# A decoder layer on one core: the value projection begins first, and the four pool weight groups are fused between its tiles 1 to 5

## The chip, the cores and the metric

The kernel runs on one core of one Trainium2 chip. The metric is the device time of one execution in microseconds (us). Three runs of the kernel before gave 2354.69, 2355.07 and 2358.67 us; their median, 2355.07 us, is the time before. A core has five engines with queues of their own: TensorE (PE in the profile; its weight loads are PEld), VectorE (DVE), ScalarE (ACT), GpSimd (POOL) and SyncE (SP), which here only issues DMAs. Each engine works through its queue in order and waits on semaphores for the others.

## The reference

One layer of a hybrid decoder. 16 meta tokens go ahead of 2048 tokens of width 1024, all are layer-normed, and one projection gives q, k, v, the forget logits, two gates and the pool input. Attention with a forget bias and a causal pooling run side by side, are gated, and go through one output projection and a second layer norm. What the change touches is the first norm, the v columns of the projection and the pool's per-group weights:

```python
h = jnp.concatenate([meta, x], axis=1)
h = layer_norm(h, ln_in_g, ln_in_b)
...
h = jnp.einsum('bld,dc->blc', x, w_in)
q, k, v, f_logit, g_att, u, g_pool = jnp.split(h, SPLITS, axis=-1)
...
    outs.append((hi - lo) / cnt - u32[:, :, sl])
d = jnp.stack(outs, axis=2)
y = jnp.einsum('blgc,gce->blge', d, w_pool.astype(jnp.float32))
```

The trailing mean is linear, so the kernel multiplies the pool input's columns of `w_in` by `w_pool` ahead of time, group by group, and projects straight into the mapped channels. This is the fusing that the change moves: for each of the four groups a 1024 x 256 matrix times a 256 x 256 one.

## The kernel before

**Numbers in two parts.** All products are in fp32 built from two parts: `split` writes a high part with ScalarE (`hi`) and the remainder, source less high part, with VectorE (`lo`), or with GpSimd where the call says so. `mm3` then issues three matmuls (high x high, high x low, low x high). Low x low is left out.

**Order.** The class `Ordered` chains the instructions of TensorE, VectorE, ScalarE and GpSimd to the order in which the code issues them. SyncE is not chained: the framework's scheduler sets the order of the DMAs. All five queues then run in order. A tile taken from a pool with `bufs=n` waits until the tile n turns earlier has been read. Nearly every instruction is recorded through one helper, so the profile gives nearly all of them line 86; they are told apart by their tiles.

**The stage that the change touches**, in the order of the code:

1. Fusing. `fuse_load` brings the weights of all four groups into tiles of their own (`wp`: 256 x 256; `wu`: two of 128 x 1024), `fuse_split` makes the parts `ph`, `pl`, `uh`, `ul`, and `fuse_mm` issues 48 matmuls of 256 columns a group into four PSUM tiles `d`, which ScalarE and VectorE copy in turn to `o` (or `vs`) for the DMA to `wupd`. The splits of the next group, the norms of the first three token tiles and the splits of the value weights `wv` (`wvh`, `wvl`) are placed between the four.
2. The first value half. Tokens are held transposed in `hh` and `hl` (high and low part, 8 slabs of 128 channels by 2064 tokens each). `ln_norm(i)` normalises token tile i (statistics `bst` and `mv` on VectorE, the root `rs` on ScalarE, `rs` and `nb` on VectorE, the scaling of `xt` on ScalarE, then gain and bias on GpSimd), `ln_turn(i)` transposes it on TensorE into `tr` and splits `tr` into `hh` and `hl`. `v_tile(0, wts, i)` multiplies 128 tokens by 512 value columns: 8 channel slabs times three matmuls of 512 columns into one of two tiles `d`; ScalarE and VectorE split that into `vs`, a DMA takes it to `vd`. In step i of the loop stand the transposes of token tile i + 1, the norm of i + 3 and value tile i. Value tile i needs token tiles i - 1 and i, since the 16 meta tokens shift them. There are 16 tiles of 128 tokens and a 17th of 16 tokens, for which the same 24 matmuls are issued.
3. The second value half: the weights of the other 512 columns are loaded to three tiles `wst` and split, and 17 value tiles follow without transposes.
4. The forget logits `zc`, then the jobs of the projections, the attention and the output; the change leaves them alone.

Of the kernel before, what the change touches and what calls it, by code (L numbers as in the profile page):

```python
# [9 lines left out]
F32 = mybir.dt.float32  # L10
# [30 lines left out]
def kernel(  # L41
# [147 lines left out]
    with ExitStack() as vscope:  # L189
        vpool = pool(vscope, "vpool")  # L190
# [21 lines left out]
        def ln_norm(i):  # L212
# [11 lines left out]
            nc.vector.scalar_tensor_tensor(  # L224
                out=nb[:n], in0=mv[:n, 0:1], scalar=-1.0, in1=rs[:n], op0=ALU.mult, op1=ALU.mult
            )
            nc.scalar.activation(
                out=xt[:n], in_=xt[:n], func=AF.Identity, scale=rs[:n], bias=nb[:n]
            )
            for op, row in ((ALU.mult, g_bc), (ALU.add, b_bc)):  # L230
                nc.gpsimd.tensor_tensor(out=xt[:n], in0=xt[:n], in1=row[:n], op=op)
# [26 lines left out]
        def v_tile(half, wts, kt):  # L258
            n = min(P, L - P * kt)
            ps = dense()  # L260
            sl = slice(P * kt, P * kt + n)
            for k in range(KT):
                mm3(ps[:n], hh[:, k, sl], hl[:, k, sl], wts[k][0], wts[k][1], k == 0, k == KT - 1)
            vs = vslot().rearrange("p (h a e) -> p h a e", h=8, a=2)
            pv = ps[:n].rearrange("p (h e) -> p h e", e=DH)
            split(vs[:n, :, 1, :], vs[:n, :, 0, :], pv)
# [5 lines left out]
        fscope = ExitStack()  # L272
        fz = pool(fscope, "fz", side="right")

        def fuse_load(g):
            wp = fz.tile([P, 2, 256], F32, tag="wp", name="wp", bufs=4)
            dma(wp, wpool[g])
            us = [wp]
            for k in range(2):
                us.append(fz.tile([P, D], F32, tag="wu", name="wu", bufs=8))  # L280
                dma(us[-1], wut[2 * g + k])
            return us

        def fuse_split(us, r):
            def one(i, u):
                shape, tag = ([P, 2, 256], "p") if i == 0 else ([P, D], "u")
                h_, l_ = (
                    fz.tile(shape, F32R, tag=tag + t, name=tag + t, bufs=2 if i == 0 else 4)
                    for t in "hl"
                )  # L290
                split(h_, l_, u, nc.gpsimd if i == 2 else None)
                r.append((h_, l_))

            return [lambda i=i, u=u: one(i, u) for i, u in enumerate(us)]

        def fuse_mm(g, ws, us, pieces):
            raw = [
                f32(vslot()) if g == 3 else fz.tile([P, D], F32, tag="o", name="o", bufs=6)
                for _ in range(2)
            ]  # L300
            os = [t.rearrange("p (k b e) -> p k b e", k=4, b=2) for t in raw]
            n = -(-len(pieces) // 4)

            def evac(kp, ps):
                pv = ps.rearrange("p (a b e) -> p a b e", a=2, b=2)
                dst = os[kp // 2][:, 2 * (kp % 2) : 2 * (kp % 2) + 2]
                if kp % 2:
                    nc.vector.tensor_copy(dst, pv)
                else:
                    nc.scalar.copy(out=dst, in_=pv)  # L310

            last = None
            for kp in range(4):
                ps = dense()
                for s in range(2):
                    dsl = slice(P * (2 * kp + s), P * (2 * kp + s + 1))
                    for k in range(2):
                        mm3(
                            ps[:, 256 * s : 256 * (s + 1)], us[k][0][:, dsl], us[k][1][:, dsl],
                            ws[0][:, k], ws[1][:, k], k == 0, k == 1,  # L320
                        )
                if last:
                    evac(*last)
                last = (kp, ps)
                for f in pieces[n * kp : n * (kp + 1)]:
                    f()
            evac(*last)
            for b in range(2):
                for q in range(2):
                    dma(wupd[2 * g + b][:, 4 * q : 4 * q + 4, :], os[q][:, :, b, :])  # L330
# [3 lines left out]
        raws = {0: fuse_load(0)}  # L334
        ln_load(-1)
        raws[1] = fuse_load(1)
# [3 lines left out]
        raws[2] = fuse_load(2)  # L340
        ln_load(1)
        raws[3] = fuse_load(3)
        ln_load(2)
        sts = deque()
        for k in range(KT):
            sts.append(fz.tile([P, 512], F32, tag="wv", name="wv", bufs=KT))
            dma(sts[-1], wv[0, k])
        dma(wfs, wf)
        dma(bf_t, b_forget)
        dma(psc_t, pool_scale)  # L350
        hot = []
        for f in fuse_split(raws.pop(0), hot):
            f()
        wts = []
        for g in range(4):
            us = hot
            ws = us.pop(0)
            hot = []
            pieces = []
            if g + 1 < 4:  # L360
                pieces += fuse_split(raws.pop(g + 1), hot)
                pieces.append(lambda: ln_norm(g - 1))
            if g >= 2:
                pieces += [lambda: wts.append(wv_split(sts.popleft()))] * 4
            fuse_mm(g, ws, us, pieces)
        fscope.close()
        htp = pool(phase_a, "htp", side="right")
        hh = htp.tile([P, KT, L], F32R, tag="hh", name="hh")
        hl = htp.tile([P, KT, L], F32R, tag="hl", name="hl")
        ln_turn(-1)  # L370
        ln_load(3)
        ln_turn(0)
        ln_norm(2)
        split(wfr[:, :, 0:H], wfr[:, :, 32 : 32 + H], wfs)
        for i in range(NKT):
# [8 lines left out]
            if i == 16:  # L384
                wts1 = [wv_split(sts.popleft())]
                sts.append(wv_load(1, 3))
            v_tile(0, wts, i)
            if i == 15:
                lnscope.close()
                wq = pool(phase_a, "wq", side="right")  # L390
        wts = wts1
        for k in range(1, KT):
            wts.append(wv_split(sts.popleft()))
            if k + 3 < KT:
                sts.append(wv_load(1, k + 3))
        for kt in range(NKT):
# [4 lines left out]
            v_tile(1, wts, kt)  # L401

# [826 lines left out]
```

## Time and profile before

| what | value |
| --- | --- |
| median of three runs | 2355.07 us |
| the profiled execution: time, span of its trace | 2353.42 us, 2351.7 us |
| granted TensorE clock over that execution | 0.994 of full |
| span busy: TensorE, VectorE, ScalarE, GpSimd | 97%, 64%, 41%, 30% |
| first value matmul, its place in the span | 56.87 us |
| transposes of token tile 6 (step 5 of the loop) begin | 91.01 us |

The span and the profiled time differ by 1.7 us, which lie outside the trace. A row of the timeline has the start, the busy time, the engine, the line, the operation, what is written from what is read with its shape, the count (xN), and in brackets the idle time ahead of it with what ended it. The busy time of one matmul is longer than the distance between the starts of two, because they are pipelined: the distance is what a stream of them costs. A row of the stretches has the bounds, the length, the busy time of each engine with the count of instructions, the granted clock, the share of time that the DMA engines were busy, and GB/s. A row of the chain of waits has a start, a length, and what the chain that ended last was doing there.

### The profile page before, as it was taken

Reading aid. Unit: us, or ns where it says so; the run is one execution under the profiler, and the core shown is the slowest. Engines: PE = TensorE matmul, PEld = TensorE weight load, DVE = VectorE, ACT = ScalarE, POOL = GpSimd, SP = SyncE. Lnnn points to the kernel's source line nnn. Section 1 sums busy time; section 2 is a strip of 40 time slices with the busy share of each in tenths; the row PEclk is TensorE's granted clock in tenths of the full one; section 3 lists DMA queues with packets and bytes.
Section 4 is the critical chain, followed back from the end, with each engine's and each line's share of the span. In section 5 each row is a group of like instructions: output and inputs, shape, how many; then the busy total and the mean of one; then the engine's idle time right before and its main releaser. Section 6 shows DMA issues by size and latency. Waiting matters only on the chain.

```text
span 2351.7 us, 32595 instructions
## 1 busy us (share of the span) xinstructions
PE 2289.3 (97%) x11450; PEld 1924.1 (82%) x11450; DVE 1501.9 (64%) x2372; ACT 959.9 (41%) x1813; POOL 716.8 (30%) x528
## 2 busy tenths in 40 slices
PE   6999999999999999999999999999999999998998
PEld 5878799999999999999888677777777777776787
DVE  6641146755766567656634488778788878877357
ACT  4431221212212212121111587777778777776000
POOL 4740021212313414140001235444453544444000
PEclk8999999999999999999999999999999999999999
DMA  7853222222222222222212857566666667555965
GB/s 252 265 175 90 69 90 70 84 63 92 91 62 91 78 70 91 62 95 80 82 65 71 219 170 226 162 210 175 186 189 187 208 173 228 169 164 164 300 193 165
DMA packets 317507, 333.59 MB, mean 142 GB/s; under 512 B 27744, under 2 KB 241072, under 8 KB 317312
## 3 DMA queue, kind: packets, MB, share of 16 engines
q1 hardware_dynamic: 317344, 331.51, 46.2%
q8 instruction: 91, 1.49, 0.3%
q14 instruction: 72, 0.59, 0.1%
HBM read 207.43 MB, written 124.00 MB: 141 GB/s over the span
## 4 chain that ended last, share of the span: by engine, by line
PE 89%; DVE 3%; DMA 3%; ACT 2%; issue 2%; POOL 1%; SPq 0%; DVEq 0%; ACTq 0%; POOLq 0%
PE d L86 61%; PE s L86 11%; PE yo L86 7%; PE mx L86 6%; PE xo L86 5%; POOL tu L86 1%; DVE pl L86 1%; PE tr L86 1%; ACT ph L86 1%; POOL araw L86 1%; DMA wst<-in_wout_dram 0%; ACT s L86 0%; DMA wu<-in_wut_dram 0%; DMA g_bc<-in_ln_in_g_dram 0%; DVE acc L86 0%
## 5 line engine op out<-in xcount | busy, mean ns | idle before, releaser
L86 PE MATMUL d<-hh,wh 128*128 128x412 f32 (+2 forms) x1472 | 543.8, 369 | 0.0
L86 PE MATMUL d<-hl,wh 128*128 128x412 f32 (+2 forms) x1472 | 538.2, 366 | 0.0
L86 PE MATMUL d<-hh,wl 128*128 128x412 f32 (+2 forms) x1472 | 537.9, 365 | 0.0
L86 DVE TENSOR_TENSOR pl<-s,ph 128x512 fp32r<-128x512 f32 (+2 forms) x576 | 375.4, 664 | 147.0 <-ACT s L86 134.2
L86 DVE TENSOR_REDUCE mxs<-mx 128x1 f32<-128x912 f32 (+14 forms) x416 | 359.5, 865 | 85.6 <-PE mx L86 75.8
L86 ACT ACTIVATE ph<-s 128x512 fp32r<-128x512 f32 (+2 forms) x576 | 335.2, 582 | 170.1 <-PE s L86 157.8
L86 PE MATMUL d<-wh,xm 128*128 128x512 f32 x1024 | 352.1, 400 | 4.5 <-DMA xm<-xa 3.7
L86 ACT ACTIVATE s<-s 128x512 f32<-128x512 f32 (+2 forms) x576 | 332.7, 578 | 0.0
L86 PEld LDWEIGHTS d<-hl,wh 128*128 128x128 f32 x1472 | 277.6, 189 | 24.8
L86 PEld LDWEIGHTS d<-hh,wh 128*128 128x128 f32 x1472 | 276.8, 188 | 23.2
L86 PEld LDWEIGHTS d<-hh,wl 128*128 128x128 f32 x1472 | 276.6, 188 | 23.4
L86 PE MATMUL s<-qa,ka 68*128 68x512 f32 (+4 forms) x704 | 257.9, 367 | 19.1 <-DVE pl L86 18.8
L86 POOL TENSOR_TENSOR wl<-wst,wh 128x1024 fp32r<-128x1024 f32 x40 | 96.3, 2407 | 571.4 <-ACT wh L86 545.8
L86 PE MATMUL s<-qb,kb 128*128 128x512 f32 (+4 forms) x704 | 244.8, 351 | 0.0
L86 PE MATMUL xo<-ph,vt 128*128 128x512 f32 (+3 forms) x640 | 232.7, 367 | 0.0
L86 POOL TENSOR_TENSOR tu<-ph 128x512 f32<-128x512 f32 x144 | 191.2, 1330 | 135.3 <-ACT ph L86 118.8
L86 PEld LDWEIGHTS d<-wh,xm 128*128 128x128 f32 x1024 | 192.3, 189 | 42.3 <-issue 2.9
L86 PE MATMUL yo<-pl,vt 128*66 128x512 f32 (+3 forms) x640 | 223.3, 365 | 1.1 <-ACT c L86 1.1
L86 PE MATMUL d<-wl,xm 128*128 128x512 f32 x512 | 204.3, 399 | 0.0
L86 PE MATMUL mx<-ka,qa 66*128 66x512 f32 (+5 forms) x704 | 197.9, 347 | 3.4 <-ACT qa L86 3.4
L86 PEld LDWEIGHTS s<-qa,ka 68*128 68x128 f32 (+1 forms) x704 | 127.8, 182 | 73.3 <-DVE pl L86 31.1
L86 DVE TENSOR_TENSOR mx<-mx,mask_q 128x128 f32<-128x128 f32 x256 | 76.6, 299 | 117.4 <-PE mx L86 115.0
(140 smaller groups left out, 3091.5 us busy)
## 6 DMA issues: line engine op xcount, KB each, us to landing
xm<-xp SPq DMA_DIRECT2D x32, 1024.0 KB
xm<-xa SPq DMA_DIRECT2D x20, 1024.0 KB
vd<-vs SPq DMA_DIRECT2D x32, 512.0 KB
vt<-vd SPq DMA_DIRECT2D x64, 256.0 KB
qb<-kqd SPq DMA_DIRECT2D x64, 256.0 KB
xa<-am SPq DMA_DIRECT2D x32, 512.0 KB
xp<-pm SPq DMA_DIRECT2D x32, 412.0 KB
kqd<-lo SPq DMA_DIRECT2D x64, 206.0 KB
```

The costliest lines, as they stand in the source:

```text
L86: return in_order(f(*a, **k))
```

## The change

The norm and the value projection now stand first, and `hh` and `hl` are allocated at the start.

- **Start.** The queue of loads begins with the meta tokens, token tile 0, the gain and bias rows and the eight value weights, which land in tiles that are free at that time (`wst`, a tile of the `xt` pool called `wraw`, and both `vs`). The norms of the meta tokens, of token tiles 0 and 1 have gain and bias on VectorE; from token tile 2 on GpSimd has them as before.
- **Fusing.** Step i of the loop, for i = 1 to 4, holds the transposes of token tile i + 1 (in step 1 those of tile 2 come behind the value tile), the norm of token tile i + 2, `fuse_feed(i - 1)`, value tile i, and `fuse_mm(i - 1)`. `fuse_feed` loads a group as five pieces of 128 x 512 (0: `w_pool`; 1 and 2: the first slab's two halves; 3 and 4: the second's) through the three tiles `wst`, so the load of piece 3 waits for the split of piece 0 and that of piece 4 for the split of piece 1. The parts go to the last 1024 token columns of `hh` and `hl`, which no token tile needs before step 7. Every low part is VectorE's. `fuse_mm` has the same 48 matmuls a group in two PSUM tiles `fz` of 1024 columns: the first half needs pieces 0, 1 and 3, the second 0, 2 and 4. ScalarE copies each half to a `vs` tile.
- **Norms.** In step 5 two norms are made up (tiles 7 and 8); later steps have that of i + 3 as before.
- **16-row tiles.** `v_rest` takes the place of the 17th value tile of each half: `hs` holds the 16 tokens' high parts in columns 0 to 15 and the low parts in columns 32 to 47, two matmuls a slab (16 in place of 24) give all four products, and the two row groups are added. During the first of them the second half's weights are split (`each`); five of these weights are loaded ahead rather than three.

The core of the diff:

```diff
+        def v_rest(half, wts, hs, each):
+
+            ps = dense()
+            for k in range(KT):
+                for t in range(2):
+                    mm(
+                        ps[:48], hs[:, k, :], wts[k][t],
+                        start=k == 0 and t == 0, stop=k == KT - 1 and t == 1,
+                    )
+                each(k)
...
+        def fuse_feed(g):
...
+            def step(i):
+                split(pieces[i][0], pieces[i][1], raw[i])
+                if i + 3 < 5:
+                    load(i + 3)
...
-            if i + 1 < 16:
+            if 2 <= i < 15:
                 ln_turn(i + 1)
-            if i + 3 < 16:
-                ln_norm(i + 3)
+            if 1 <= i < 5:
+                ln_norm(i + 2)
+                parts = fuse_feed(i - 1)
+            elif i:
+                for t in (7, 8) if i == 5 else (i + 3,):
+                    if t < 16:
+                        ln_norm(t)
...
             v_tile(0, wts, i)
+            if i < 2:
+                ln_turn(i + 1)
+            if 1 <= i < 5:
+                fuse_mm(i - 1, parts)
```

How this moves the queues is seen at three places. First VectorE at the start of the program. Before, its first rows are the splits of the pool weights and the first copy of a fused tile:

```order
L86 TENSOR_TENSOR pl<-wp,ph 128x512
L86 TENSOR_TENSOR ul<-wu,uh 128x1024
L86 TENSOR_TENSOR pl<-wp,ph 128x512
L86 TENSOR_TENSOR ul<-wu,uh 128x1024
L86 COPY o<-d 128x512
L86 BN_STATS bst<-xt 16x6 x2
```

With the change, behind the statistics of two norms, they are the gains and biases of the meta tokens (16 rows) and of token tile 0, then value weights, then the low parts of the first transposes:

```order
L86 TENSOR_TENSOR xt<-xt,g_bc 16x1024
L86 TENSOR_TENSOR xt<-xt,g_bc 128x1024
L86 TENSOR_TENSOR xt<-xt,b_bc 16x1024
L86 TENSOR_TENSOR xt<-xt,b_bc 128x1024
L86 TENSOR_TENSOR wvl<-wst,wvh 128x512
L86 TENSOR_TENSOR wvl<-wraw,wvh 128x512
L86 TENSOR_TENSOR hl<-tr,hh 128x4x16 x2
L86 TENSOR_TENSOR hl<-tr,hh 128x4x128 x2
```

The pool weights' splits have left the start, and four sums of 1024 columns now stand ahead of the first transposes.

Second, ScalarE's queue in one step of the loop. Before (steps 1 and 2), between two value tiles' `vs`:

```order
L86 CAST vs<-d 128x8x64
L86 CAST hh<-tr 128x4x128 x2
L86 ACTIVATE rs<-mv,eps_t 128x1
L86 ACTIVATE xt<-xt,nb,rs 128x1024
L86 CAST vs<-d 128x8x64
```

With the change (step 3: behind the copies of group 1, to those of group 2):

```order
L86 CAST vs<-d 128x8x64
L86 COPY vs<-fz 128x1024 x2
L86 CAST hh<-tr 128x4x128 x2
L86 ACTIVATE rs<-mv,eps_t 128x1
L86 ACTIVATE xt<-xt,nb,rs 128x1024
L86 CAST hl<-wst 128x512 x5
```

The two copies of the group before now stand ahead of the transposes' high parts, of the norm, and of the five high parts of the next group (`hl<-wst` here are pieces whose place lies in `hl`).

Third, SyncE's queue around the same step (`wupd_75` and `wupd_76` are group 1's results). Before, a step had a token tile, a value tile and the normed tokens:

```order
L86 DMA xt<-in_x_dram 128x1024
L86 DMA vd_58<-vs 128x8x128
L86 DMA hd<-xt 128x1024
L86 DMA vd_58<-vs 128x8x128
L86 DMA xt<-in_x_dram 128x1024
L86 DMA hd<-xt 128x1024
```

With the change:

```order
L86 DMA wst<-in_wpool_dram 128x512
L86 DMA wst<-in_wut_dram 128x512 x2
L86 DMA vd_58<-vs 128x8x128
L86 DMA wupd_75<-vs 128x4x128
L86 DMA wupd_76<-vs 128x4x128
L86 DMA xt<-in_x_dram 128x1024
L86 DMA wupd_75<-vs 128x4x128
L86 DMA wupd_76<-vs 128x4x128
L86 DMA wst<-in_wut_dram 128x512 x2
L86 DMA hd<-xt 128x1024
```

The first three pieces of the next group stand ahead of this step's results, its pieces 3 and 4 (the second `wst<-in_wut_dram 128x512 x2`) behind them.

More of the change, by code (lines that the diff above doesn't have):

```diff
@@ L270, in v_tile @@
             )
[L272 to L278, printed above, removed]
-            for k in range(2):
[L280 to L316, printed above, removed]
+        def v_tile(half, wts, kt):
+            ps = dense()
+            sl = slice(P * kt, P * (kt + 1))
+            for k in range(KT):
+                mm3(ps, hh[:, k, sl], hl[:, k, sl], wts[k][0], wts[k][1], k == 0, k == KT - 1)
+            v_out(half, kt, P, ps)
@@ L320, in fuse_mm @@
                             ws[0][:, k], ws[1][:, k], k == 0, k == 1,
                         )
[L322 to L330, printed above, removed]
+                o = f32(vslot())
+                nc.scalar.copy(out=o, in_=ps)
```

171 lines of the change are left out of this document (115 added, 56 removed).

## The prediction

> **What bounds the kernel now.** The first view read is the chain that ended last, by engine:
>
> ```profile
> PE 89%; DVE 3%; DMA 3%; ACT 2%; issue 2%; POOL 1%; SPq 0%; DVEq 0%; ACTq 0%; POOLq 0%
> ```
>
> TensorE sets the time almost throughout, so what the change is worth lies where TensorE waits. The second view is the table of stretches, cut at the stages that change: the fusing, the first value half, the second.
>
> ```profile
> 0.00:56.80 56.80, 35.04 (x215) 32.24 (x216) 39.18 (x47) 27.02 (x40) 28.65 (x21) 0.90 0.75 253
> 56.80:166.70 109.90, 108.63 (x523) 87.04 (x523) 58.78 (x117) 45.30 (x76) 67.29 (x28) 0.99 0.71 230
> 166.70:266.20 99.50, 96.49 (x409) 73.87 (x409) 16.32 (x24) 14.95 (x25) 3.35 (x4) 1.00 0.34 101
> ```
>
> The first number behind the length is TensorE's busy time: it idles for 21.8 us of the first 56.8 and hardly later. The third view, its waits over the first 320 us, says for whom:
>
> ```profile
> PE d L86 <- DVE o L86: 10.2, 4, 5.1
> PE d L86 <- ACT uh L86: 6.8, 2, 6.0
> ```
>
> So the fusing is fed too slowly by VectorE and ScalarE, before any value tile runs. The change wants to hide that feeding behind value tiles. The question is whether five splits, a norm and a load fit behind one tile.
>
> **Prices of TensorE.** From the chain of waits in the steady loop, and the copies that follow the 16th tile, the second half's first, and its last:
>
> ```profile
> 111.36 5.56 PE d L86 x24
> 116.92 0.87 PE tr L86 x8
> 161.14 0.59 ACT L86 CAST vs<-d 128x512 fp32r<-128x512 f32 x1 [4.97 <-PE d L86]
> 168.62 2.60 DMA wst<-in_wv_dram
> 177.34 0.59 ACT L86 CAST vs<-d 128x512 fp32r<-128x512 f32 x1 [1.55 <-PE d L86]
> 266.29 0.57 ACT L86 CAST vs<-d 16x512 fp32r<-16x512 f32 x1 [4.95 <-PE d L86]
> ```
>
> A value tile costs 5.56 us (0.232 a matmul), its transposes 0.87, a step 6.44. From the 16th tile's end to the stage's end pass 266.2 - 161.1 = 105.1 us. A fused group's matmuls:
>
> ```profile
> 27.56 0.39 PE L86 MATMUL d<-ph,uh 128*128 128x256 f32 x1 [4.30 <-DVE o L86]
> 27.78 0.28 PE L86 MATMUL d<-pl,uh 128*128 128x256 f32 x1
> ...
> 34.65 0.28 PE L86 MATMUL d<-pl,uh 128*128 128x256 f32 x1
> 34.77 0.28 PE L86 MATMUL d<-ph,ul 128*128 128x256 f32 x1
> 40.15 0.58 PE L86 MATMUL d<-ph,uh 128*128 128x256 f32 x1 [5.10 <-DVE o L86]
> 44.79 0.41 PE L86 MATMUL d<-ph,uh 128*128 128x256 f32 x1
> 45.01 0.41 PE L86 MATMUL d<-pl,uh 128*128 128x256 f32 x1
> ```
>
> Start to start is 0.12 us at full clock and 0.21 behind the idle 5.1 us; behind the idle 4.3 us the clock was still full at first. Half a group (24) is 2.9 us, or 5.1 at the low clock; a whole group 5.7.
>
> **What is surely gained: 8.7 us, all behind the 16th tile.** The 16-row tiles have 16 matmuls for 24, 3.7 us each. The second half's weights are split during the first of these; before, its first tile took 177.2 - 166.7 = 10.5 us for 5.56, waiting for loads of the 2.60 us shown. Five weights lie ready now, and the last two are loaded and split by the time that slabs 6 and 7 come up, 0.7 us a slab. So 3.7 + 16 x 5.56 + 3.7 = 96.4 against 105.1.
>
> **The start.** The first load and the transfer rate:
>
> ```profile
> 0.81 0.39 SPq L86 DMA_DIRECT2D wp<-in_wpool_dram  x1
> 3.40 0.62 ACT L86 CAST ph<-wp 128x512 fp32r<-128x512 f32 x1 [1.32 <-DMA wp<-in_wpool_dram]
> 0.00:20.00 20.00, 10.74 (x61) 9.66 (x61) 8.90 (x13) 9.87 (x12) 6.75 (x13) 1.00 0.92 343
> ```
>
> 256 KB are usable 2.6 us after the issue, and then 343 GB/s flow: meta tokens at 3, token tile 0 at 4.5, gain and bias (1.6 MB in all) at 7.5, weights until 13.5. The norm's rows, and those of a 1024-column sum on VectorE and of the high parts:
>
> ```profile
> 4.89 1.04 ACT L86 CAST uh<-wu 128x1024 fp32r<-128x1024 f32 x1 [0.87 <-DMA wu<-in_wut_dram]
> 5.97 1.23 DVE L86 TENSOR_TENSOR ul<-wu,uh 128x1024 fp32r<-128x1024 f32 x1 [1.23 <-ACT uh L86]
> 54.03 1.07 ACT L86 CAST hh<-tr 128x512 fp32r<-128x512 f32 x2 [1.29 <-PE tr L86]
> 61.91 1.28 DVE L86 TENSOR_TENSOR hl<-tr,hh 128x512 fp32r<-128x512 f32 x2
> 63.11 1.27 DVE L86 BATCH_NORM_STATS2 bst<-xt 128x6 f32<-128x512 f32 x2
> 65.39 1.25 ACT L86 ACTIVATE xt<-xt,nb,rs 128x1024 f32<-128x1024 f32 x1 [0.43 <-DVE nb L86]
> 66.71 2.41 POOL L86 TENSOR_TENSOR xt<-xt,g_bc 128x1024 f32<-128x1024 f32 x1 [2.38 <-ACT xt L86]
> 69.19 2.38 POOL L86 TENSOR_TENSOR xt<-xt,b_bc 128x1024 f32<-128x1024 f32 x1
> ```
>
> Statistics to scaling take 2.3 us, scaling 1.2. Two norms in a row: statistics from 3 to 7.5, scalings to 9.9, four sums of 1.2 on VectorE until 13.3, transposes, high part: the first value matmul at 16 instead of 56.87. It starts at the low clock, so tile 0 ends near 22. VectorE meanwhile makes the transposes' low parts, six low parts of weights, then statistics, wait and two sums of token tile 1: 27. Behind that stand, still ahead of token tile 1's split, the statistics of token tile 2 (to 29.3) and on ScalarE its scaling (to 30.6). **Value tile 1 starts at 31, with TensorE idle most of the time since 22.** It ends at 38. Group 0 waits for its pieces by the chain below, which starts from token tile 1's low parts (32.5): it ends at 50.
>
> **The four fused steps: the largest term.** Here VectorE and GpSimd meet:
>
> ```profile
> 4.05 0.69 DVE L86 TENSOR_TENSOR pl<-wp,ph 128x512 fp32r<-128x512 f32 x1 [2.10 <-ACT ph L86]
> 8.65 2.35 POOL L86 TENSOR_TENSOR ul<-wu,uh 128x1024 fp32r<-128x1024 f32 x1 [6.04 <-ACT uh L86]
> 9.12 2.43 DVE L86 TENSOR_TENSOR pl<-wp,ph 128x512 fp32r<-128x512 f32 x1 [1.92 <-ACT ph L86]
> 40.84 2.38 POOL L86 TENSOR_TENSOR xt<-xt,g_bc 128x1024 f32<-128x1024 f32 x1 [1.37 <-ACT xt L86]
> 41.31 6.45 DVE L86 TENSOR_TENSOR wvl<-wv,wvh 128x512 fp32r<-128x512 f32 x4 [1.22 <-ACT wvh L86]
> 43.30 2.70 POOL L86 TENSOR_TENSOR xt<-xt,b_bc 128x1024 f32<-128x1024 f32 x1
> ```
>
> The same low part takes 0.69 us alone, and 2.43 when it starts inside a GpSimd sum: it ends 0.55 behind that sum's end (11.00). Four of them beside two such sums take 6.45 for 2.5. So the two engines take turns when VectorE reads two tiles of SBUF.
>
> The Trainium skill, "GPSIMD Engine Reference", Specifications, says that GpSimd's SBUF interfaces are shared with VectorE and that instructions with two SBUF inputs contend. The rows agree (2.43 against 0.69). By that rule the term below stands; were it wrong, the second rival's sum would hold.
>
> A fused step, counted from the end of the previous group's last matmul, with the queues in the order that they have now: ScalarE's copy of 1024 columns 1.1 (estimate from its 1.04), both high parts of the transposes until 2.2, second low part 2.8, statistics to scaling 5.0, scaling 6.3. GpSimd takes the gain until 8.7. Low part of piece 0, held by it, 9.4; GpSimd's bias 11.8; low part of piece 1 12.4. Piece 3's load is issued at 9.4, lands 2.6 later, and is split at 13.4; piece 4's is issued at 12.4, lands at 15.0, and is split at 16.4. TensorE is done with transposes and value tile at 6.4. The first half group runs from 13.4 to 16.3 (18.5 at the low clock, with 6 to 7 us idle ahead of it), the second from there: **19.3 to 21.4 us, taken as 20.4** (the middle, since idle stretches of 4.3 and 5.1 us ended in different clocks), against 12.1 (6.44 + 5.7) without waits.
>
> Behind TensorE's wait stand the next transposes and value tile; behind ScalarE's wait for pieces 3 and 4 stand `vs`, the next two copies and the next high parts; behind VectorE's stand the low parts of `vs` and of the next transposes. TensorE waits for all of these only through the next group, so nothing catches up in between.
>
> The Trainium skill, "TensorE: Matmul & The Clock Gate", Part 1, puts the clock to half behind an idle window of about 3.4 us. By it the period is 21.4 and the sum 3 us more. The rows agree at 5.1 us idle, and at 4.3 us not at once.
>
> Steps 2 to 4 thus last from 50 to 111.2. Step 5 takes 6.44 to 117.6. Then token tile 7 is late: its norm stands only in step 5, its chain (11.2 by the same count, two GpSimd sums behind the scaling) ends at 122.4. Steps 6 to 15 take 10 x 6.44 - 0.87 (step 15 has no transposes) = 63.5, so the 16th tile ends at 185.9. Before it was 161.1.
>
> **Sum.** +24.8 - 8.7 = +16.1 us; from the profiled execution's 2353.42 us that is 2369.5. The median of the runs is 1.65 above that execution, which gives **2371.0 us**. What follows the stage only shifts.
>
> At no cost I set the forget weights' loads, which move in SyncE's queue (beside 5.56 us of matmuls a step; 0.4 us of queue each if not), and `hs` (a memset and two casts behind tiles 14 and 15; under 1 us). For the ScalarE copy of 1024 columns out of PSUM no row stands: from 1.04 (SBUF) to twice 0.59, worth 0.1 a step either way. Loads that queue behind the 512 KB transfers of the same steps are unseen: nothing at best, at worst 512 KB at 343 GB/s, 1.5 us, for each of the two in series, 3 us a step.
>
> **Rivals.** *Same chain, slow loads*: those 3 us in all four steps, +12: 2383 us. For it speaks that a step moves 3.8 MB (five pieces, four results of 256 KB each, and three times 512 KB); against it, 20 us at 343 GB/s carry 6.9. Chance 0.13.
>
> *No taking turns in this place*: if the low parts find GpSimd idle, pieces 0 and 1 are split at 7.5 and 8.1, piece 3 at 11.4, the first half ends at 14.3, the second at 17.2. Three steps by 3.2 and group 0 by 2.4 take off 12: 2359, barely slower. Against it: ScalarE's order puts the scaling, and so the gain, just ahead of piece 0. Chance 0.14.
>
> *Faster, since the pieces are split during the tile's own matmuls*: a step then costs 12.1. It needs piece 3 ready at 6.4 and piece 4 at 9.3, which decides: to turn the forecast to -4.7, 21 us must go, over 5 a step, so the period must fall below 15. Three times 8.3 and about 6 in group 0 give 31 less: 2340. Against it is ScalarE's queue, which has two copies, the high parts and a norm ahead of piece 0 (6.3 us), and the load of piece 3 that needs piece 0's slot. Chance 0.06.
>
> *The late norms hide*: if token tiles 1 and 7 come in time, 8 and 4.9 us fall away, and +16.1 becomes +3.2: 2358, no change that can be told. Against it: both norms stand in queues that the code orders, behind work that is counted above. Chance 0.04.
>
> **How the numbers follow.** The forecast, +9 to +24, has 0.63. Two runs can tell about 0.2% (4.7 us) apart. Slower: forecast 0.63, slow loads 0.13, and most of the second rival (0.09) make 0.85; same: the rest of that rival and the last, 0.09; faster 0.06. The range reaches from the second rival's time, 2358, to the slow loads' 2384; what is left out is the faster case, the last, and tails, about 0.15.
>
> **What would show it.** First value matmul at 15 to 17 us and value tile 1 at 29 to 32, with VectorE's sums between. In steps 2 to 4 the gap in TensorE ahead of `fz` is 5 to 8 us, released by low parts; `hh<-wst` and `hl<-wst` rows on VectorE of 2 to 3 us beside `xt<-xt,g_bc` and `xt<-xt,b_bc`; a step lasts 19 to 22. Step 6 begins with about 5 us for GpSimd. The 16th tile ends at 181 to 191, and the stage 96.4 later. I am wrong if `fz` follows its value tile within 3 us.

## The result: 1.04% slower, and the profile after

The changed kernel takes 2379.59 us (median of 4 runs, 2379.02 to 2384.33) against 2355.15 for the kernel before in the same session: a ratio of 1.0104, 95% interval 1.0092 to 1.0116, that is +24.4 us. The forecast was +16 (2371.0 in a range of 2358 to 2384). The profiled execution took 2379.65 us, its span is 2377.8 against 2351.7.

The chain that ended last, by engine, in the changed kernel:

```profile
PE 87%; DVE 4%; DMA 3%; ACT 2%; issue 2%; POOL 2%; SPq 0%; DVEq 0%; ACTq 0%; POOLq 0%
```

TensorE's share fell by two points; VectorE and GpSimd took one each. Where, the table of stretches shows. It is cut at value tile 1, at the start of steps 2 to 6, and at the end of the 16th tile; behind each length stand the busy times of PE, PEld, DVE, ACT and POOL, then TensorE's granted clock, the DMA share and GB/s:

```profile
0.00:31.50 31.50, 10.91 (x49) 8.65 (x49) 21.44 (x41) 14.37 (x24) 2.83 (x12) 0.94 0.71 250
31.50:50.40 18.90, 17.19 (x80) 14.71 (x81) 12.36 (x16) 7.23 (x12) 8.91 (x4) 0.75 0.62 197
50.40:71.75 21.35, 15.19 (x83) 12.99 (x82) 10.69 (x13) 7.81 (x12) 5.01 (x2) 0.84 0.66 207
71.75:94.65 22.90, 16.26 (x82) 13.90 (x81) 10.76 (x13) 7.81 (x12) 5.03 (x2) 0.78 0.61 184
94.65:115.77 21.12, 15.55 (x82) 13.35 (x81) 10.69 (x13) 7.82 (x12) 5.02 (x2) 0.84 0.56 176
115.77:128.25 12.48, 6.60 (x34) 5.20 (x33) 6.98 (x13) 5.53 (x8) 4.74 (x3) 0.93 0.46 134
128.25:194.30 66.05, 66.05 (x313) 54.62 (x314) 33.03 (x66) 25.61 (x44) 38.64 (x17) 0.96 0.65 203
194.30:290.70 96.40, 96.40 (x417) 75.78 (x415) 17.32 (x26) 15.97 (x27) 3.41 (x4) 1.00 0.37 109
```

In each of the three fused steps in the middle TensorE is busy 15 to 16 us of 21 to 23, at a clock of 0.78 to 0.84. The 16th tile ends at 194.3 us where it was 161.1 (+33.2). The stage behind it takes 96.4 us where it was 105.1 (-8.7). Together +24.5; the rest of the span difference of 26.1 lies behind the stage, in code that the change doesn't touch.

TensorE's waits over the first 320 us (engine, tile, what was waited for: us, times, longest):

```profile
PE tr L86 <- DVE xt L86: 16.5, 2, 11.7
PE fz L86 <- DVE hh L86: 9.6, 6, 2.4
PE tr L86 <- POOL xt L86: 5.9, 1, 5.9
PE fz L86 <- ACT hh L86: 3.9, 2, 2.2
PE fz L86 <- DVE hl L86: 3.7, 2, 2.2
PE fz L86 <- ACT hl L86: 2.9, 1, 2.9
```

The waits for `o` and `uh` are gone, and larger ones took their place: the first norms, the pieces of the fused groups (20.1 us in four rows of `fz`), and token tile 7. What feeds the pieces, the timeline of step 2 shows (start, duration, instruction, and in brackets the idle time ahead and who ended it):

```profile
58.24 2.35 POOL L86 TENSOR_TENSOR xt<-xt,g_bc 128x1024 f32<-128x1024 f32 x1 [16.30 <-ACT xt L86]
58.70 5.78 DVE L86 TENSOR_TENSOR hh<-wst,hh 128x512 fp32r<-128x512 f32 x3 [1.81 <-ACT hh L86]
59.24 0.38 PE L86 MATMUL fz<-hh 128*128 128x256 f32 x1 [2.23 <-ACT hh L86]
...
60.66 2.67 POOL L86 TENSOR_TENSOR xt<-xt,b_bc 128x1024 f32<-128x1024 f32 x1
...
61.19 0.38 PE L86 MATMUL fz<-hh 128*128 128x256 f32 x1 [1.56 <-DVE hh L86]
...
63.94 0.58 PE L86 MATMUL fz<-hh 128*128 128x256 f32 x1 [2.37 <-DVE hh L86]
```

Three low parts beside two GpSimd sums take 5.78 us, where 0.69 each is the price alone. The first `fz` matmul (59.24) multiplies high parts only. The first that needs a low part starts 0.6 behind the end of the gain, the next 0.6 behind the end of the bias.

What the forecast hadn't counted stands in ScalarE's rows: the copies of each group's second half, in groups 0 to 3:

```profile
51.90 1.01 ACT L86 COPY vs<-fz 128x1024 f32<-128x1024 f32 x1 [3.26 <-DMA vd<-vs]
...
73.91 1.02 ACT L86 COPY vs<-fz 128x1024 f32<-128x1024 f32 x1 [3.42 <-DMA vd<-vs]
...
95.49 1.01 ACT L86 COPY vs<-fz 128x1024 f32<-128x1024 f32 x1 [2.77 <-DMA vd<-vs]
...
117.04 1.01 ACT L86 COPY vs<-fz 128x1024 f32<-128x1024 f32 x1 [2.87 <-DMA vd<-vs]
```

The groups' last matmuls end where the next step starts, at 50.4, 71.75, 94.65 and 115.77. The copies start 1.5, 2.2, 0.8 and 1.3 us later, because `vs` has two slots and three users in a step: the value tile, whose result is still being written out, and two copies. That result is late for a reason of its own, as ScalarE's rows of step 2 show:

```profile
63.69 0.62 ACT L86 CAST hl<-wst 128x512 fp32r<-128x512 f32 x1 [3.98 <-DMA wst<-in_wut_dram]
...
66.89 0.62 ACT L86 CAST hl<-wst 128x512 fp32r<-128x512 f32 x1 [2.58 <-DMA wst<-in_wut_dram]
67.41 0.58 ACT L86 CAST vs<-d 128x512 fp32r<-128x512 f32 x1
```

TensorE had finished this value tile at 57.0, but in ScalarE's queue the high parts of pieces 3 and 4 stand ahead of its copy, and ScalarE waits 4.0 and 2.6 us for their loads. Behind the second copy of `fz` stand the high parts of the next transposes and the whole next chain.

And token tile 7, in the chain of waits (start, us, what):

```profile
112.71 4.23 DMA vd<-vs
...
123.43 2.34 POOL xt L86
...
125.86 2.35 POOL xt L86
...
128.25 1.97 PE tr L86 x8
130.22 7.00 PE d L86 x24
```

The first row is a result on its way out of its slot, for which the copy at 117.04 waited. GpSimd's two sums stand right in front of TensorE, and the transposes and value tile behind the idle time take 1.97 and 7.00 us for 0.87 and 5.56.

### The profile page after: what moved, and what is told of

It is laid out like the page before. It is cut to its first block, busy times and chain, and to the rows that moved or that the text cites. A ratio compares the mean times of both kernels' runs of the same rounds, so it can differ in the third digit from the quotient of the medians.

```text
span 2377.8 us, 32612 instructions
## 1 busy us (share of the span) xinstructions
PE 2296.3 (97%) x11434; PEld 1933.1 (81%) x11434; DVE 1511.2 (64%) x2385; ACT 965.4 (41%) x1823; POOL 690.7 (29%) x519
## 4 chain that ended last, share of the span: by engine, by line
PE 87%; DVE 4%; DMA 3%; ACT 2%; issue 2%; POOL 2%; SPq 0%; DVEq 0%; ACTq 0%; POOLq 0%
PE d L86 59%; PE s L86 11%; PE yo L86 7%; PE mx L86 6%; PE xo L86 5%; DMA vd<-vs 1%; POOL tu L86 1%; DVE pl L86 1%; ACT ph L86 1%; POOL araw L86 1%; PE tr L86 0%; DVE hh L86 0%; DVE hl L86 0%; DVE bst L86 0%; DMA wst<-in_wv_dram 0%
## 5 line engine op out<-in xcount | busy, mean ns | idle before, releaser
L86 POOL TENSOR_TENSOR wl<-wst,wh 128x1024 fp32r<-128x1024 f32 x40 | 96.3, 2407 | 541.6 <-ACT wh L86 515.9
```

Of the source, the lines that this page charges most:

```text
L86: return in_order(f(*a, **k))
```

## The experiments

Twelve runs, each timed beside the kernel before. "Steps" are the lengths of steps 2 to 4, from one start of transposes to the next; "16th" is when ScalarE starts to copy the 16th tile. The stage behind it takes 96.3 to 96.8 us in each of them, so "16th" is what an edit moved. It scatters by itself, too: the two profiles of the 16-row tiles alone, the same kernel, have 161.3 and 162.6.

| run | median us (range) | ratio to before, 95% interval | steps 2 to 4, us | 16th, us |
|---|---|---|---|---|
| the change | 2379.59 (2379.02 to 2384.33) | 1.0104 (1.0092 to 1.0116) | 21.3, 22.9, 21.1 | 194.3 |
| e1_rows_alone | 2346.94 (2346.05 to 2348.35) | 0.9962 (0.9947 to 0.9977) | | 161.3 |
| e2_feed_first | 2367.55 (2365.55 to 2373.51) | 1.0056 (1.0040 to 1.0073) | 18.3, 19.9, 18.5 | 181.1 |
| e3_two_more_slots | 2373.74 (2371.97 to 2374.63) | 1.0074 (1.0059 to 1.0089) | 20.3, 20.1, 20.4 | 187.5 |
| e4_result_slot | 2376.73 (2373.60 to 2383.07) | 1.0091 (1.0071 to 1.0111) | 20.0, 20.4, 20.3 | 187.5 |
| e5_norm7_early | 2375.69 (2373.36 to 2376.51) | 1.0081 (1.0066 to 1.0096) | 22.9, 21.3, 22.8 | 191.0 |
| e6_no_gain | 2368.16 (2366.71 to 2372.22) | 1.0053 (1.0038 to 1.0068) | 19.8, 19.5, 18.4 | 184.1 |
| e7_warm | 2380.28 (2378.56 to 2382.49) | 1.0099 (1.0083 to 1.0116) | 21.5, 21.5, 23.5 | 195.6 |
| e8_all_ahead | 2349.10 (2346.41 to 2350.44) | 0.9971 (0.9959 to 0.9983) | 14.3, 13.8, 14.0 | 163.1 |
| e9_start | 2350.03 (2347.45 to 2352.21) | 0.9979 (0.9970 to 0.9988) | | 165.2 |
| e10_rows_alone_again | 2347.72 (2345.47 to 2348.86) | 0.9967 (0.9956 to 0.9979) | | 162.6 |
| e11_write_later | 2347.99 (2346.59 to 2349.13) | 0.9968 (0.9956 to 0.9980) | | 161.9 |
| e12_split_between | 2344.58 (2343.32 to 2348.48) | 0.9957 (0.9945 to 0.9970) | | 158.8 |

**One half of the change alone.** The kernel before with the 16-row tiles and the five weights that lie ready; the fusing, the norms and the start stay as they were:

```diff
-        for i in range(NKT):
+        for i in range(NKT - 1):
...
+        v_rest(0, wts, hs, each)
+        wts = w1
+        for kt in range(NKT - 1):
...
+        v_rest(1, wts, hs, lambda k: None)
```

> The kernel before with one part of the change: v_rest for the 16-row tiles, five of the second half's weights loaded ahead. Fusing and norms stay as before. My theory (this part is worth 8.7 us by itself, and the loss lies wholly in the fused steps): 2346 to 2347 us, 8 to 9 below the kernel before, with the second half's first tile done 3.7 + 5.6 us behind the 16th tile. Rival (what is saved here is waited for later, at the forget logits): 2354 to 2355 us.

2346.94 us, 8.3 below before. This half is worth what the forecast gave it (8.7), so the other half (start, norms and fusing) costs 32.6: the difference between the two medians, 2379.59 - 2346.94. A repeat in another session gave 2347.72:

> The first experiment again (only the 16-row tiles and the five weights ahead, the fusing as before the change), beside the run above on the same chip, so that the two can be compared: 2345 to 2348 us.

**Taking turns: the order of norm and pieces.**

```diff
             if 1 <= i < 5:
-                ln_norm(i + 2)
                 parts = fuse_feed(i - 1)
+                ln_norm(i + 2)
```

> The changed kernel with fuse_feed ahead of ln_norm in steps 1 to 4; nothing else. Theory A (a step's length is the chain norm, GpSimd's gain, low parts of pieces, so the pieces come too late because they stand behind the norm): low parts of pieces 0 to 2 from about 4.5 us behind the previous group instead of 9, alone and 0.7 us each; the step is then held by the next token tile's GpSimd sum and lasts 16 to 18 us instead of 21 to 23: 2360 to 2366 us. Theory B (the loads of the pieces, one behind another through three slots and beside other traffic, set the step): within 3 us of the changed kernel, 2377 to 2382.

12.0 us less than the change, 1.5 us short of the first theory's range; the second theory is out. The steps lose about 3 us each, but the wait moves: the transposes of the next token tile now wait for its bias, in TensorE's timeline of this run,

```profile
67.27 1.59 PE L86 MATMUL tr<-ident,xt 128*128 128x128 f32 x8 [3.59 <-POOL xt L86]
87.13 1.10 PE L86 MATMUL tr<-ident,xt 128*128 128x128 f32 x8 [3.72 <-POOL xt L86]
105.59 1.97 PE L86 MATMUL tr<-ident,xt 128*128 128x128 f32 x8 [3.73 <-POOL xt L86]
```

since pieces 3 and 4 still wait for their loads, and the norm now stands behind them.

**Taking turns: no GpSimd sums in steps 1 to 4.**

```diff
             if 1 <= i < 5:
-                ln_norm(i + 2)
+                ln_apply(i + 2, *ln_stat(i + 2))
```

> Token tiles 3 to 6 get neither gain nor bias (GpSimd's two sums of steps 1 to 4 are left out, and the output differs); the split of the fused pieces and the rest stay. Theory: VectorE's low parts then take 0.67 us each instead of waiting for GpSimd, but the loads of pieces 3 and 4 and the two copies stay, so a step loses 1.3 to 2 us: 2372 to 2375 us. Rival (taking turns is the largest part of a step, as the second rival of the forecast had it, 3.2 us a step): 2367 us. Rival (the loads alone set the step, sharing does not matter): 2379 to 2380 us.

2368.16 us, 11.4 less than the change, close to the first rival's 2367. VectorE's rows of step 3 in this run show why:

```profile
75.38 1.90 DVE L86 TENSOR_TENSOR hl<-wst,hl 128x512 fp32r<-128x512 f32 x3 [1.82 <-ACT hl L86]
79.72 0.69 DVE L86 TENSOR_TENSOR hl<-wst,hl 128x512 fp32r<-128x512 f32 x1 [2.44 <-ACT hl L86]
```

Three low parts take 1.90 us where they took 5.78 in step 2 of the change, and then VectorE waits for ScalarE, which waits 2.67 for piece 3's load. The Trainium skill, "GPSIMD Engine Reference", Specifications, has GpSimd's SBUF interfaces shared with VectorE, with contention where a VectorE instruction has two SBUF inputs; this run agrees with it by these 1.90 against 5.78 us.

Taking turns is thus shown, but the 11.4 us are not its price alone. With the low parts earlier, the loads of pieces 3 and 4, the copy of the value tile and its write are earlier too, and ScalarE's second copy waits for its matmuls (they end at 68.4) and no longer for a slot:

```profile
68.59 1.01 ACT L86 COPY vs<-fz 128x1024 f32<-128x1024 f32 x1 [1.79 <-PE fz L86]
```

Steps 2 to 4 together are 7.7 us shorter than in the change, but only 3.1 shorter than with a third result slot (below), where the sums remain.

**Loads: a slot for each of the five pieces.**

```diff
-                return vpool.tile([P, 512], F32, tag="wst", name="wst", bufs=3)
-            return vpool.tile([P, 512], F32R, tag=kind, name=kind, bufs=KT + 1)
+                return vpool.tile([P, 512], F32, tag="wst", name="wst", bufs=5)
+            return vpool.tile([P, 512], F32R, tag=kind, name=kind, bufs=KT)
...
-            for i in range(3):
+            for i in range(5):
                 load(i)
```

(The room comes from the second half's first weight, which is split a step later.)

> The changed kernel with five tiles wst instead of three, so that all five pieces of a group are loaded ahead and none waits for a split; room comes from one pair of wvh/wvl less (the second half's first weight is split in v_rest rather than in step 15, at most 1 us). Theory A (low parts behind the norm and GpSimd set the step): the low part of piece 4 comes 2 to 3 us earlier, but the matmuls are still at the first half by then: 2377 to 2381 us. Theory B (loads through three slots set the step): 2 to 3 us less in each of four steps, 2367 to 2372 us.

5.9 us less, between the two. VectorE's row of step 3 says what is left when no load is waited for:

```profile
76.10 7.00 DVE L86 TENSOR_TENSOR hl<-wst,hl 128x512 fp32r<-128x512 f32 x5 [1.82 <-ACT hl L86]
```

All five low parts run in one piece, and still take 7.0 us for 3.4, held up by the same two sums. So as far as the low parts go, the loads of pieces 3 and 4 lay beside the taking of turns. What was gained lies elsewhere: ScalarE no longer waits for loads, the value tile of step 2 is copied 9.5 us after the step's start (17.0 in the change), and the second copy finds its slot free:

```profile
58.30 0.58 ACT L86 CAST vs<-d 128x512 fp32r<-128x512 f32 x1
...
69.31 1.01 ACT L86 COPY vs<-fz 128x1024 f32<-128x1024 f32 x1 [1.45 <-PE fz L86]
```

**The result slot.** A third `vs` slot, with room made in the same way:

```diff
-            return vpool.tile([P, 8 * P], F32R, tag="vs", name="vs", bufs=2)
+            return vpool.tile([P, 8 * P], F32R, tag="vs", name="vs", bufs=3)
```

> The changed kernel with three tiles vs instead of two (room as in the run with five tiles wst), so that ScalarE's second copy of a group does not wait until the value tile's DMA has left its slot. In the changed kernel these four copies started 1.5, 2.2, 0.8 and 1.3 us behind the group's last matmul. My theory (this wait is part of the chain of a step): 4 to 6 us less, 2373 to 2376 us. Rival (ScalarE has slack there): within 1.5 us of the changed kernel, 2378 to 2381.

The median fell by 2.9, between the two expectations, but the stage itself tells more: the 16th tile ends 6.9 us earlier, and steps 2 to 4 last 20.0, 20.4 and 20.3 us, the forecast's 20.4. The second copies of groups 2 and 3 wait for their matmuls now, and no longer for a slot; group 2's row:

```profile
89.49 1.01 ACT L86 COPY vs<-fz 128x1024 f32<-128x1024 f32 x1 [1.79 <-PE fz L86]
```

Five load tiles had done the same: its 16th tile is at 187.5 too, and its steps are 20.3, 20.1 and 20.4. The two edits cut one chain in two places (late loads, late copy of the value tile, late write, no free slot), so their gains are the same 4.6 us in steps 2 to 4 and don't add. Of the 6.9 in this run, 1.6 lie ahead of step 2, where the clock came up earlier: the transposes of token tile 2 start at 38.6, against 40.0 in the change, and they start anywhere from 38.9 to 40.0 in the profiles of the change, e5_norm7_early and e7_warm, whose code is the same up to there.

That the median kept less is the rest of the program: what follows the stage takes 2085.4 us of span in the profile of before, 2086.9 in that of the change and 2089.5 in this one, in code that no edit touches.

**Token tile 7.**

```diff
+                if i == 4:
+                    ln_norm(7)
...
-                for t in (7, 8) if i == 5 else (i + 3,):
-                    if t < 16:
-                        ln_norm(t)
+                if i + 3 < 16:
+                    ln_norm(i + 3)
```

> Only the place of one norm changes: that of token tile 7 goes from step 5 to step 4, behind the fused pieces. Theory: the 5.9 us that TensorE waits for GpSimd ahead of token tile 7's transposes go, and with them the half clock behind that wait (7.00 us for a value tile that takes 5.56, and 1.97 for transposes that take 0.87, so 2.5 us); nothing in step 4 waits for the moved norm, since it stands behind the pieces: 2371 to 2372 us, 8 below the changed kernel. Rival: the moved norm holds up step 4's own chain (ScalarE's scaling stands ahead of the tile's copies) by as much as step 5 gains: 2378 to 2381 us.

3.9 us less, half of what was expected. The wait of 5.9 in front of token tile 7 is gone, but norms that run late stay late: token tile 8 waits now, as TensorE's timeline shows (and tile 13, for 0.8),

```profile
132.63 1.09 PE L86 MATMUL tr<-ident,xt 128*128 128x128 f32 x8 [2.19 <-POOL xt L86]
```

and steps 2 to 4 together are 1.7 us longer in this profile (+1.6, -1.6, +1.7). Step 2 lies ahead of the edit, so such differences of a single step aren't the moved norm's alone. The rival was right in part: in step 4 the scaling of token tile 7 now stands ahead of the value tile's copy, which starts at 116.7 (111.3 in the change), and the second copy of group 3 starts 4.0 us behind the group's last matmul where it was 1.3.

**The low clock.** 22 matmuls of 512 columns, which no output needs, in front of each group's first half, to keep TensorE busy while it waits:

```diff
                 ps = psm.tile([P, 1024], F32, tag="mx", name="fz", bufs=2)
+                for r in range(0 if half else 22):
+                    mm(ps[:, 0:512], hh[:, r % KT, 0:P], wts[r % KT][0], start=True, stop=True)
```

> 22 more matmuls of 512 columns (about 5 us at full clock) go into the psum tile of each group's first half ahead of its own, whose values they leave alone since the first real matmul starts anew; they stand where TensorE idles. Work is only added. Theory: TensorE then meets the pieces at full clock, and a half group takes 2.9 us instead of up to 5.1: about 2 us a step are gone in four steps: 2371 to 2374 us. Rival (the low clock costs nothing, since later pieces set the end): 2378 to 2381 us, or more if the added work is in the way (up to 5 us a step, 2400).

2380.28 us: nothing gained. 88 added matmuls of 0.23 us, 20 us of TensorE's time, cost under 1 us, so deep is the idle time they fell into. But they didn't do what they were for. The stretches of step 2, in this run:

```profile
56.90:62.10 5.20, 5.20 (x24) 4.18 (x24) 3.38 (x3) 2.79 (x4) 3.67 (x2) 1.00 0.05 16
62.10:65.50 3.40, 1.35 (x7) 0.79 (x6) 3.19 (x3) 0.62 (x1) 1.44 (x1) 1.00 0.34 104
65.50:69.00 3.50, 3.50 (x18) 3.50 (x19) 1.21 (x2) 1.10 (x2) 0.00 (x0) 0.54 0.96 316
```

and, in its timeline, the longest gap:

```profile
64.14 0.38 PE L86 MATMUL fz<-hh 128*128 128x256 f32 x1 [1.69 <-DVE hh L86]
```

TensorE is busy throughout until 62.1, then 1.35 of 3.4 us while it waits for the last low part, and the clock falls to 0.54 when the half group runs. The wait right in front of the half group was left. So the run doesn't settle what a full clock would be worth. The Trainium skill, "TensorE: Matmul & The Clock Gate", Part 1, names an idle window of about 3.4 us as what brings half clock. In this run no window of that length was idle: the longest gap is 1.69 us, and the clock fell all the same. The measurement decides.

**All of it at once.** Pieces ahead of the norm, five slots, and each norm a step earlier from step 1 on:

```diff
             if 1 <= i < 5:
-                ln_norm(i + 2)
                 parts = fuse_feed(i - 1)
...
+            if i == 1:
+                ln_norm(3)
+            if i and i + 3 < 16:
+                ln_norm(i + 3)
```

> Three edits of the changed kernel at once: the fused pieces are split ahead of the norm, all five have a slot of their own (so they are loaded a step ahead), and from step 1 on each norm is made one step earlier (so that of token tile 7 is early too). Theory (a step lasts as long as its feeding takes, not TensorE's 12.1 us): with the pieces ready at the step's start a step lasts 13 to 15 us instead of 21.8, -20 to -26 in three steps, and -8 for token tile 7: 2345 to 2352 us, about what 16-row tiles alone gave. Rival (the two copies that wait for a result slot, and the scaling and GpSimd sums of the norm, still make a step of 17 to 18 us): 2357 to 2362 us.

2349.10 us, 30.5 below the change, as expected. The transposes at the starts of steps 3 to 5, in TensorE's timeline of this run, stand 13.8 and 14.0 us apart, with no wait in front:

```profile
61.89 1.04 PE L86 MATMUL tr<-ident,xt 128*128 128x128 f32 x8
...
75.72 1.04 PE L86 MATMUL tr<-ident,xt 128*128 128x128 f32 x8
...
89.68 1.03 PE L86 MATMUL tr<-ident,xt 128*128 128x128 f32 x8
```

That is more than the edits gave apart (12.0, 5.9, and 3.9 with only one norm moved; here each norm is moved). With the pieces first, the loads are what is late next, and with these ready, the norm is; each hid behind the other. The three recover nearly all of the 32.6 us that the other half of the change costs.

**The start, and one queue.** On top of that, token tile 2's norm no longer stands in front of token tile 1's split, group 0's pieces are split ahead of it, and group 0 is fused ahead of token tile 2's transposes (those of token tile 3 move behind value tile 2):

```diff
-        ln_norm(2)
...
+            if i == 0:
+                ln_turn(1)
+                parts = fuse_feed(0)
+                ln_norm(2)
...
             if 1 <= i < 5:
                 fuse_mm(i - 1, parts)
+            if i == 1:
+                ln_turn(2)
```

> The kernel of the run before it (pieces first, five slots, norms a step ahead) with the start set in another order: the norm of token tile 2 no longer stands ahead of token tile 1's split, group 0's pieces are split ahead of it, and group 0 is fused ahead of the transposes of token tile 2. Theory (the 8.6 us between tile 0 and value tile 1 are VectorE's and ScalarE's queues, of which token tile 2's statistics and scaling are 2 to 4): value tile 1 starts at 28 to 29 us instead of 31.5, group 0 follows it without token tile 2, and the 16th tile ends 3 to 6 us earlier: 2343 to 2346 us, at or a little below 16-row tiles alone. Rival (the norm of token tile 2 is only late elsewhere, since GpSimd's two sums and the split now stand in front of value tile 2): 2349 to 2352 us.

2350.03 us, no gain: the rival's time. The timeline shows the new wait:

```profile
41.56 5.05 SPq L86 DMA_DIRECT2D hd<-xt  x2
...
46.71 0.39 SPq L86 DMA_DIRECT2D vd<-vs  x1
...
50.97 1.01 ACT L86 COPY vs<-fz 128x1024 f32<-128x1024 f32 x1 [6.74 <-DMA vd<-vs]
...
52.52 0.80 PE L86 MATMUL d<-wvh,hh 128*128 128x512 f32 x1 [9.83 <-ACT hh L86]
```

The result of value tile 1 is ready at 44.0 us, but SyncE's queue has two writes of normed tokens in front, and the second waits for GpSimd until 46.3. So the slot comes free late, the second copy of group 0 waits 6.74, and behind it on ScalarE stand the high parts for value tile 2. The next run sets only that order right:

```diff
+                if i in (2, 3):
+                    tc.add_manual_dep(ins.ins, last_on["vd"].ins.name, ...)
```

> The kernel with the start in another order, with one thing changed: SyncE issues the result of value tile 1 ahead of the writes of normed token tiles 2 and 3, not behind them (the second of them waited for GpSimd's bias until 46.3 us). Theory: the result leaves its slot 2.7 us earlier, so the second copy of group 0 and the high parts behind it are 2.7 us earlier, and so is value tile 2: 2347 to 2348 us. Rival (the slot comes free no earlier, since the write itself takes its 4.3 us and others stand beside it): 2349.5 to 2351 us.

2347.99 us, and the 16th tile ends 3.2 us earlier: as expected. The last run lets the high parts pass the waiting copy, in all four fused steps (and the writes of normed token tiles 4 and 5 stand behind their step's result, too):

```diff
                 nc.scalar.copy(out=o, in_=ps)
+                if half == 0:
+                    mid()
...
-                fuse_mm(i - 1, parts)
+                fuse_mm(i - 1, parts, lambda: ln_turn(i + 1))
```

> The kernel of the run before it; in each of the four fused steps the transposes of the next token tile and their split stand between the two half groups, so ScalarE makes the high parts ahead of the second copy, which waits for a result slot. Theory (that copy's wait is what is left of the fused steps, 1.8 us in each and 9.8 in front of value tile 2): TensorE runs through from value tile 1 on, a fused step takes 12.1 to 12.6 us, the 16th tile ends at 149 to 152 us instead of 165, and the time is 2334 to 2341 us, below 16-row tiles alone. Rival (the transposes now wait for GpSimd's bias in front of the second half group, and the second copy's wait comes back as a wait for the pieces' low parts behind it): 2345 to 2350 us.

2344.58 us, between the two. From the transposes of token tile 3 to those of tile 4 now pass 12.1 us (56.57 to 68.69), as TensorE alone needs; but the step before takes 14.9 and the one behind 13.5, and the 16th tile ends at 158.8, not 149 to 152. At the start the rival was right, the transposes wait for GpSimd's bias and run at a low clock behind that wait (1.97 for 1.04 us):

```profile
41.71 1.97 PE L86 MATMUL tr<-ident,xt 128*128 128x128 f32 x8 [3.38 <-POOL xt L86]
...
56.57 1.04 PE L86 MATMUL tr<-ident,xt 128*128 128x128 f32 x8
```

This is the fastest of all, and beats both kernels: 0.9957 of before (0.9945 to 0.9970). The 16-row tiles alone, at 0.9962 and 0.9967, cannot be told from it.

## Why the forecast was right, and where it was short

**The gain of 8.7 us behind the 16th tile** was right: 96.4 us in the table of stretches, and 8.3 us by the first experiment.

**The start** was right: value tile 1 starts at 31.5 (31), group 0 ends at 50.4 (50). The parts were not: value tile 1 took 8.5 us for 7, and group 0 made it up.

**The four fused steps: right mechanism, a term left out.** VectorE and GpSimd take turns as the chain had it, and the chain can be followed in VectorE's rows. The half group's stream needs the low part of piece 3, which was to be ready 13.4 us after the start of the step. These rows of steps 2 to 4 of the change end with it:

```profile
64.41 0.68 DVE L86 TENSOR_TENSOR hl<-wst,hl 128x512 fp32r<-128x512 f32 x1
...
80.70 6.45 DVE L86 TENSOR_TENSOR hl<-wst,hl 128x512 fp32r<-128x512 f32 x4 [1.81 <-ACT hl L86]
...
102.34 6.39 DVE L86 TENSOR_TENSOR hh<-wst,hh 128x512 fp32r<-128x512 f32 x4 [1.88 <-ACT hh L86]
```

They end 14.7, 15.4 and 14.1 us after the steps' starts. The forecast's chain began with ScalarE's copy, at 1.1 us; but it let the second copy start at once, and it waits for a result slot for 1.5, 2.2 and 0.8 us behind the last matmul. Less those waits the low part is ready at 13.2 in all three. From there to the end of the group pass 6.7, 7.5 and 7.0 us, between the forecast's 5.9 and 8.0 for the two clocks. So the steps were 21.3, 22.9 and 21.1 instead of 20.4; less the waits they are 19.9, 20.7 and 20.3, and with a third slot 20.0, 20.4 and 20.3. That term is +4.2 in the sum. The forecast had seen that `vs` stands behind ScalarE's wait for pieces 3 and 4, but it put no price on the write that holds the slot after that.

**Token tile 7** was right, and 3.8 us cheap with what stands behind it. Its chain took 12.5 us for 11.2, and the 1.3 more are again the second copy's wait. Behind the idle time the transposes and the value tile ran at a low clock, 1.97 + 7.00 for 0.87 + 5.56, which the sum didn't have, though it counted half clock as possible behind other waits: 2.5 us more.

**The sum.** 0.4 at the start, 4.2, 1.3 and 2.5 are the 8.4 us by which the 16th tile came later than the 185.9 foretold; +16.1 and 8.4 make +24.5, and the medians differ by 24.4. (2369.5 and 1.65 are 2371.2, not 2371.0.) Nearly all of the error is thus two terms, a full slot and a clock. The forecast gave 0.63 to +9 to +24, and +24.4 lies just above that. It lies in the wider range by the room that was left for slow loads, which did not come about; that it fell inside is luck to that extent.

**The signs.** The alternating rows of VectorE and GpSimd, the wait in front of step 6 and the 96.4 us came as named. TensorE's idle time ahead of the half groups is 6.2, 6.6 and 5.6 us a step, within the 5 to 8, but in three pieces with single matmuls between. The 16th tile's 181 to 191 and step 3's 22.9 were missed, for the terms above. And by its letter the sign that was to prove the forecast wrong came: the first `fz` follows its value tile within 3 us, after 2.2, 2.9 and 1.6. That matmul multiplies high parts only, which no GpSimd sum holds up; the sign should have named the first that needs a low part.

**The rivals.** *Slow loads* (2383) came nearest to the time, for another reason: pieces 3 and 4 reached ScalarE 2.5 to 3.2 us after their issue, for the 2.6 of the forecast, and with all five loaded a step ahead the steps are 20.1 to 20.4, no shorter than the forecast's chain. What the waiting for loads cost came through the result slot. *No taking turns* was wrong as a forecast. Its 12 us and the 11.4 measured agree by luck: it had 3.2 us a step, its count took full clock where the forecast took the middle, and the run gave 1.5, 3.4 and 2.8 us, of which the slot's waits are the larger part. *Faster, the pieces hidden* needed a period below 15. The changed kernel was far from it; pieces first, more slots and earlier norms together reach 14.0, and this place then costs about as much as the fusing stage that it replaces. *The late norms hide* did not happen in either place.

What stays open: what a full clock in the half groups would be worth, since the added matmuls didn't keep it up; and what the taking of turns costs by itself, since the edit that leaves the sums out frees the result slot too. The 3.1 us in three steps between the run without sums and the run with a third slot are an estimate of it.

## What to carry to other kernels

Work that is moved to lie beside other work takes that work's queues, slots and ports with it. Before hiding something behind a tile, list for each engine and each pool of slots what stands there already, and count as late whatever stands behind a wait. And undo causes together as well as one by one: what gave 3.9 to 12.0 us apart gave 30.5 together, because each cause hid behind another. The reverse holds as well: a wait that goes when a tile gets more slots doesn't show that this tile was its cause. Here two more load tiles and one more result tile cured the same wait.

## What the runs showed that was not expected

- The clock fell to 0.54 behind 3.4 us in which TensorE was busy for 1.35, right after 5.2 us of unbroken work.
- A result of 512 KB held its slot for 4.2 us behind the issue (the first row of the chain above).
- What follows the value stage takes 2085.4 to 2090.0 us of span in these profiles, in unchanged code: more than some of the edits were worth. The end of the stage in the trace leaves this out, though it too differed by 1.3 us between two profiles of the same kernel.
